# Weight blocks of two large experts placed between those of five small ones in the expert stage of a two-layer trunk, and the scatter of an expert's rows moved into the next unit

## The chip, the cores and the metric

The kernel runs on one core of one Trainium2 chip. The metric is the device time of one execution in microseconds, as the median of several runs. The kernel before took 1100.32 us (three runs, 1099.13 to 1101.1).

## The reference: what is computed

A trunk of two layers on 256 frames of 1024 channels, all in float32, batch 1. Layer 0 has attention and pooling with a dense SwiGLU, layer 1 a state-space mixer with a mixture of eight experts, and a norm ends it. Only the mixture matters here:

```
def swiglu(h, w1, w3, w2):
    return (jax.nn.silu(h @ w1) * (h @ w3)) @ w2

def moe_swiglu(h, router_w, router_b, w1, w3, w2):
    xf = h.reshape(b * s, d)                       # 256 x 1024
    top_vals, top_idx = lax.top_k(logits, TOP_K)   # 2 of 8
    gates = jax.nn.softmax(top_vals, axis=-1)
    ...
    for e in range(N_EXPERTS):
        ye = swiglu(xf, w1[e], w3[e], w2[e])       # D_FF = 2816
        out = out + combine[:, e:e + 1] * ye
# x = x + moe_swiglu(rms_norm(x)); the output is rms_norm(x)
```

## The kernel before, in words

All weights are streamed from device memory in tiles of 1 MB, each 128 partitions by 2048 values, by the queue of SP. The tiles go in turn into a ring of 17 buffers, all named raw here. An expert's weights are 33 tiles (`NBLK` is 11), so the eight experts make 264 loads.

**Rooms.** Instead of all 256 frames, an expert works on the frames that chose it, gathered into a fixed number of slots. The experts are renumbered by their counts (`by_count`): positions 0 to 5 have room for 64 frames and are called small, positions 6 and 7 have 128 and are called large. A loop behind the stage takes what doesn't fit; it isn't entered with these inputs. `Rows.gather` (L1212) makes the gathered rows x with one-hot matmuls, `Rows.scale` (L1226) the gates; `hold` does both for several experts at once. `hold([0], 64)` comes ahead of the stage, the one for the other small ones after unit 3 of expert 0, the one for the large ones after unit 3 of the next.

**Units.** The hidden width of 2816 is worked through in blocks of H = 512 (five of them) and one of 256. A full block has four tiles of w1 and w3 and two of w2, a half block three tiles. A small expert takes a block as one unit: 64 slots fill half of the columns of the array, which the profile shows as the shape 128*64. A large expert takes a full block as two half units of 256 hidden columns each, with 128 slots (128*128); both halves read the same four tiles, and each one tile of w2. A unit is

- `moe_in` (L1247): 16 steps over the channels into one PSUM bank p; then ScalarE (L1253) and VectorE (L1254) make g = silu(.) * (.) of 128x256 values;
- `moe_T` (L1261): two transposes of g into a bank t; ScalarE copies it to hT (L1263);
- `moe_out` (L1276): hT times w2, accumulated over the expert's units into one bank y (small) or two (large).

The function `turn` puts a unit's transposes into the middle of the next unit's `moe_in` (the argument `between`), and `tail` puts its `moe_out` behind that `moe_in`, so that ScalarE and VectorE have time for g and hT. The contexts `after(...)` only say what an instruction may not precede; the rest of the order on an engine is settled when the kernel is built, by when the build reckons that operands will be there.

**The end of an expert.** `slots_T` (L1284) transposes the one-hot matrix, `scatter` copies the banks y to SBUF as yf (ScalarE L1299 or L1302, VectorE L1300 or L1303) and multiplies by the one-hot matrix (L1312): frames 0 to 127 go into two banks y (`acc`) that are kept through the whole stage and were started with the residual x by `residual` (L1291); frames 128 to 255 go into two banks t, which VectorE adds to xt (L1316). In the last expert both halves are accumulated upon the residual in PSUM, and `final` (L1332 to L1355) works from there. PSUM has four banks y, two p and two t.

The experts run one after the other, in the order of positions 0, 1, 7, 2, 3, 6, 4, 5.

Of the kernel before, what the change touches and what calls it, by code (L numbers as in the profile page):

```python
# [20 lines left out]
NE = 8  # L21
# [7 lines left out]
NF = 5  # L29
# [9 lines left out]
def trunk_kernel(tc, x, par, cb, w_pool, wt, we, final_norm, out):  # L39
# [17 lines left out]
    with es:  # L57
# [1060 lines left out]
        order = [0, 1, 7, 2, 3, 6, 4, 5]  # L1118

# [174 lines left out]
        def scatter(PT, ys, acc, o1):  # L1294

            last = o1 is not None
            yf = tab.tile([128, 2, 512], F32, name="yf", tag="t2")
            if len(ys) == 1:
                sc.copy(yf[:, 0, 0:256], ys[0][:, 0:256])  # L1299
                ve.tensor_copy(yf[:, 0, 256:512], ys[0][:, 256:512])  # L1300
            else:
                sc.copy(yf[:, 0], ys[0])  # L1302
                ve.tensor_copy(yf[:, 1], ys[1])  # L1303
            o1 = o1 or [ttile(), ttile()]
            for tb, os in ((0, acc), (1, o1)):
                for nb in range(2):
                    if len(ys) == 1:
                        r = slice(64 * nb, 64 * nb + 64)
                        lhs, rhs = PT[r, tb], yf[r, 0]
                    else:  # L1310
                        lhs, rhs = PT[:, tb], yf[:, nb]
# [48 lines left out]
        def experts(todo, at):  # L1360

            acc = residual([ytile(), ytile()], 0)
            o1 = []
            prev = None

            def turn(st, behind):

                with after(behind):
                    st["h"] = moe_T(st["g"])
                return moe_T.last  # L1370

            def tail(st, B=None):
                n, u, h, ys, R, i, W = (st[k] for k in ("n", "u", "h", "ys", "R", "i", "W"))
                end = u == st["last"]
                moe_out(ys, h, B or [W.load(k) for k in st["B"]], R, u == 0, end)
                if end:
                    scatter(st["PT"], ys, acc, o1 if n == len(todo) - 1 else None)

            for n, p in enumerate(todo):
                W = Weights(p)  # L1380
                w = room(p) if len(todo) > 1 else 128

                units = []
                for t0 in range(0, 3 * NBLK, 6):
                    H = min(512, (3 * NBLK - t0) // 3 * 256)
                    if w == 64:
                        units.append((t0, H, 0, [t0 + H // 128 + k for k in range(H // 256)]))
                    else:
                        units += [(t0, H, h, [t0 + H // 128 + h]) for h in range(H // 256)]
                PT = None  # L1390
                for u, (t0, H, half, out_tiles) in enumerate(units):
                    if half == 0:
                        A = [W.load(t0 + s) for s in range(H // 128)]
                    if u == 0:
                        R, i = at(p)
                    g1 = moe_in(A, H, half, R, i, lambda mm: prev and turn(prev, mm))
                    if prev is not None:
                        with after(moe_in.last):
                            tail(prev)
                    if u == 0:  # L1400
                        ys = [ytile() for _ in range(w // 64)]
# [148 lines left out]
```

## Time and profile before

| | |
|---|---|
| median of three runs | 1100.32 us |
| the profiled execution | 1100.34 us |
| its span | 1098.3 us |
| PE busy, DMA | 97%, 311 GB/s over the span |
| expert stage (gather of expert 0 to the last scatter) | 433 to 1086 us |
| the two large experts | about 578 to 711 and 828 to 962 us |
| mean granted clock of TensorE | 0.99 of full speed |

The profile is of one execution. PE is the row of TensorE's matmuls, PEld that of its weight loads, DVE is VectorE, ACT ScalarE, POOL GpSimd, SP the engine whose queue issues the loads. The records of PE's matmuls carry modelled ends: a group's start is observed, its end lies a little beyond the start of the next one. Steps between starts are therefore the safe measure. A float32 matmul of the program shows as two matmuls (x8 for four) in the trace, a transpose as one. A square bracket behind a row gives the idle time ahead of it and what ended it.

### The profile page before, as it was taken

To read this page: it belongs to the slowest core of one execution; us is meant where nothing else is said; L and a number is where in the kernel's file an instruction comes from. 1 tells how busy PE (TensorE), PEld (TensorE's weight loads), DVE (VectorE), ACT (ScalarE), POOL (GpSimd) and SP (SyncE) were. 2 spreads that over 40 slices of the span, in tenths; PEclk is the share of its full clock that TensorE was granted. 3 is DMA by queue.
4 is the path that set the end of the run, shared out by engine and by line. 5 is a ranking of instruction groups with operands and counts; after the bars stand their busy time and mean duration, and the time that the engine had idled before them with its cause. 6 is when DMAs were issued, how large, how long until landed. Compare 5 with 4: busy or idle time off the path is not lost.

```text
span 1098.3 us, 13420 instructions
## 1 busy us (share of the span) xinstructions
PE 1061.1 (97%) x5139; PEld 606.6 (55%) x5139; DVE 388.1 (35%) x767; ACT 303.4 (28%) x563; POOL 139.0 (13%) x132
## 2 busy tenths in 40 slices
PE   8999999999999899999999999999998999999994
PEld 8977888888887778343343444333333444333331
DVE  6787968578779865110010000100100000000102
ACT  6474746644485551111010000000000000000101
POOL 2500999300003201000000000000000000000000
PEclk9999999999999999999999999999999999999998
DMA  6534545435443278799999987999999999999994
GB/s 248 228 115 154 189 156 192 154 116 208 161 148 136 78 295 356 322 427 425 428 425 428 427 320 317 420 407 427 426 427 427 428 426 384 387 387 426 427 425 164
DMA packets 48119, 341.63 MB, mean 311 GB/s; under 512 B 5296, under 2 KB 5936, under 8 KB 6832
## 3 DMA queue, kind: packets, MB, share of 16 engines
q1 hardware_dynamic: 47616, 340.02, 76.2%
q8 instruction: 42, 0.69, 0.2%
q10 hardware_dynamic: 432, 0.68, 0.2%
q14 instruction: 29, 0.24, 0.1%
HBM read 339.63 MB, written 1.05 MB: 310 GB/s over the span
## 4 chain that ended last, share of the span: by engine, by line
PE 74%; DMA 13%; DVE 5%; issue 4%; ACT 3%; POOL 1%; SPq 0%; POOLq 0%; ACTq 0%; DVEq 0%
PE p L1247 28%; PE y L1276 13%; DMA raw<-in_we_dram 12%; PE p L125 4%; PE p L126 4%; PE p L124 4%; PE y L124 4%; PE y L126 4%; PE y L125 4%; PE t L1261 1%; DVE hl L120 1%; PE t L1212 1%; ACT hl L119 1%; PE y L1312 1%; PE t L699 1%
## 5 line engine op out<-in xcount | busy, mean ns | idle before, releaser
L1247 PE MATMUL p<-raw,x 128*64 128x512 f32 (+2 forms) x1504 | 403.6, 575 | 1.9 <-DMA raw<-in_we_dram 1.9
L1247 PEld LDWEIGHTS p<-raw,x 128*64 128x64 f32 (+1 forms) x1504 | 144.7, 151 | 213.0 <-issue 196.6
L1254 DVE SCALAR_TENSOR_TENSOR g<-p,rs,g 128x256 f32<-128x256 f32 (+1 forms) x58 | 27.3, 470 | 541.0 <-ACT g L1253 541.0
L1276 PE MATMUL y<-raw,hT 128*64 128x512 f32 (+1 forms) x704 | 199.6, 594 | 2.0 <-DMA raw<-in_we_dram 1.4
L120 DVE TENSOR_TENSOR hl<-raw,hl 128x1024 fp32r<-128x1024 f32 x114 | 161.6, 1438 | 38.0 <-ACT hl L119 36.6
L119 ACT CAST hl<-raw 128x1024 fp32r<-128x1024 f32 x114 | 118.1, 1052 | 73.1 <-PE y L126 50.3
L1276 PEld LDWEIGHTS y<-raw,hT 128*64 128x64 f32 (+1 forms) x704 | 70.6, 150 | 119.2 <-issue 111.9
L1263 ACT COPY hT<-t 128x256 f32<-128x256 f32 (+1 forms) x58 | 20.9, 361 | 364.1 <-PE t L1261 364.1
L1338 POOL TENSOR_TENSOR fr<-fr,mhalf 128x1 f32<-128x1 f32 x2 | 1.1, 548 | 659.5 <-DVE fr L1337 659.5
L1253 ACT ACTIVATE g<-p,rs 128x256 f32<-128x256 f32 (+1 forms) x58 | 26.8, 462 | 176.8 <-PE p L1247 176.8
L124 PE MATMUL p<-hl,h1h 128*128 128x512 f32 x176 | 70.2, 399 | 0.1
L126 PE MATMUL p<-hl,h1l 128*128 128x512 f32 x176 | 69.3, 394 | 0.4 <-DVE h1l L207 0.4
L125 PE MATMUL p<-hl,h1h 128*128 128x512 f32 x176 | 69.6, 395 | 0.0
L126 PEld LDWEIGHTS p<-hl,h1l 128*128 128x128 f32 x176 | 33.1, 188 | 8.0 <-DVE h1l L207 0.9
L125 PEld LDWEIGHTS p<-hl,h1h 128*128 128x128 f32 x176 | 33.1, 188 | 7.1 <-DVE hl L120 0.3
L124 PEld LDWEIGHTS p<-hl,h1h 128*128 128x128 f32 x176 | 33.2, 188 | 6.6 <-ACT h1h L204 0.3
L1261 PEld LDWEIGHTS t<-ident,g 128*128 128x128 f32 x110 | 12.8, 141 | 40.3 <-issue 35.8
L124 PE MATMUL y<-hl,th 128*128 128x512 f32 x88 | 34.9, 396 | 0.0
L126 PE MATMUL y<-hl,tl 128*128 128x512 f32 x88 | 34.5, 393 | 0.0
L125 PE MATMUL y<-hl,th 128*128 128x512 f32 x88 | 34.2, 388 | 0.0
L124 PE MATMUL y<-h0h,hl 128*128 128x256 f32 x96 | 27.2, 284 | 0.0
L126 PE MATMUL y<-h0h,hl 128*128 128x256 f32 x96 | 27.2, 285 | 0.0
(406 smaller groups left out, 1247.0 us busy)
## 6 DMA issues: line engine op xcount, KB each, us to landing
raw<-in_we_dram SPq DMA_DIRECT2D x264, 1024.0 KB, 17.9
raw<-in_wt_dram SPq DMA_DIRECT2D x57, 1024.0 KB, 4.8
xt<-in_x_dram SPq DMA_DIRECT2D x2, 512.0 KB, 4.4
CB<-in_cb_dram SPq DMA_DIRECT2D x1, 1024.0 KB, 4.8
raw<-in_final_norm_dram SPq DMA_DIRECT2D x1, 512.0 KB, 18.3
out_dram<-raw SPq DMA_DIRECT2D x2, 256.0 KB, 3.5
out_dram<-raw ACTq DMA_DIRECT2D x2, 256.0 KB, 2.3
wpl<-in_w_pool_dram SPq DMA_DIRECT2D x1, 256.0 KB, 9.3
```

The costliest lines, as they stand in the source:

```text
L119: sc.copy(h.a[k][:, c], r[:, d])
L120: ve.tensor_sub(lo.a[k][:, c], r[:, d], f32(h.a[k][:, c]))
L124: pe.matmul(o, lh, rh, start=start, stop=False)
L125: pe.matmul(o, lh, rl, start=False, stop=False)
L126: pe.matmul(o, ll, rh, start=False, stop=stop)
L699: pe.matmul(t[0:32, k * 64:(k + 1) * 64], Bm[:, k, i].rearrange("p a b -> p (a b)"), Wu[:, c0 + k, i, 0:4].rearrange("p a b -> p (a b)"), ...
L1247: mm = pe.matmul(o[:, 0:2 * n].rearrange("p (w f) -> p w f", w=2), R.lhs(i, kc), a[:, kc % (KC // len(A)), :, h * n:h * n + n], start=kc = ...
L1253: sc.activation(g1, p[:, 0:n], AF.Silu, scale=R.rs[:, i, 0:1])
L1254: ve.scalar_tensor_tensor(g1, p[:, n:2 * n], R.rs[:, i, 1:2], g1, op0=OP.mult, op1=OP.mult)
L1261: moe_T.last = pe.transpose(t[:, f * 128:(f + 1) * 128], g1[:, f * 128:(f + 1) * 128], ident)
L1263: sc.copy(h, t[:, 0:n])
L1276: pe.matmul(o, h[:, j * w:j * w + w], B[c // 2][:, v:v + 512], start=first and c == 0, stop=last and c == m - 1)
```

## The change

The eight experts no longer run one after the other from position 1 on. `units` lists an expert's units; behind expert 0 the list `seq` takes the 30 units of experts 1 to 5 in turn, and spreads among them the 12 blocks of experts 7 and 6, each with its halves together. `experts` walks this list, with a small and a large expert under way at the same time, each with its banks y. The loads are issued in the same new order. Both holds now lie in expert 0, after its units 2 and 4.

`scatter` makes the copies yf as before, but hands back its matmuls as a function `add`, which `turn` calls behind the next unit's transposes. They go to two banks t and two banks y, and VectorE adds all four results to xt; no bank is kept for the sums. `residual` is called only at the end, for both halves of the frames, ahead of the last expert's scatter, which accumulates in PSUM as before. The loop for what doesn't fit is adapted. Line numbers of the stage's helpers are two lower (L1245, L1259, L1274, L1282, L1289, L1310, VectorE's adds L1313).

```diff
@@ -1115,8 +1115,6 @@
-        order = [0, 1, 7, 2, 3, 6, 4, 5]
...
@@ -1291,9 +1289,8 @@
-        def scatter(PT, ys, acc, o1):
-
-            last = o1 is not None
+        def scatter(PT, ys, sums):
+
             yf = tab.tile([128, 2, 512], F32, name="yf", tag="t2")
...
-            o1 = o1 or [ttile(), ttile()]
-            for tb, os in ((0, acc), (1, o1)):
-                for nb in range(2):
...
-                    pe.matmul(os[nb], lhs, rhs, start=tb == 1 and not last, stop=tb == 1 or last)
-            if not last:
-                for nb in range(2):
-                    xo = xt[:, 1, nb * 512:nb * 512 + 512]
-                    ve.tensor_add(xo, xo, o1[nb])
+            def add(banks):
+                for tb in range(2):
+                    for nb in range(2):
+                        o = sums[tb][nb] if sums else banks[tb]()
...
+                        i = pe.matmul(o, lhs, rhs, start=not sums, stop=True)
+                        if not sums:
+                            xo = xt[:, tb, nb * 512:nb * 512 + 512]
+                            ve.tensor_add(xo, xo, o)
+                return i
+
+            return add
...
@@ -1357,55 +1357,62 @@
-        def experts(todo, at):
-
-            acc = residual([ytile(), ytile()], 0)
-            o1 = []
...
+        def turn(st, behind):
+
+            with after(behind):
+                st["h"] = moe_T(st["g"])
+            if turn.left is None:
+                return moe_T.last
+            with after(moe_T.last):
+                i = turn.left((ttile, ytile))
+            turn.left = None
+            return i
...
+        def experts(seq, at, ahead):
+
             prev = None
...
                 if end:
-                    scatter(st["PT"], ys, acc, o1 if n == len(todo) - 1 else None)
...
+                    turn.left = scatter(e["PT"], e["ys"], sums)
+
+            for st in seq:
+                p = st["p"]
+                if st["u"] == 0:
+                    ex[p] = dict(W=Weights(p))
+                e = ex[p]
+                if st["half"] == 0:
+                    e["A"] = [e["W"].load(st["t0"] + s) for s in range(st["H"] // 128)]
...
+                st["g"] = moe_in(e["A"], st["H"], st["half"], e["R"], e["i"], lambda mm: prev and turn(prev, mm))
+                if prev is not None:
+                    with after(moe_in.last):
+                        tail(prev)
...
             turn(prev, moe_in.last)
-            o1 += residual([ttile(), ttile()], 1)
-            return prev, tail, [acc, o1]
+            return prev, tail, lambda k: ex[prev["p"]]["W"].load(k)
...
-            if (n, u) == (0, 3):
+            if (p, u) == (0, 2):
                 hold(list(range(1, NF + 1)), 64)
-            if (n, u) == (1, 3):
+            if (p, u) == (0, 4):
                 hold(list(range(NF + 1, NE)), 128)
...
+        few = [x for p in range(1, NF + 1) for x in units(p, 64)]
+        many = [x for p in range(NE - 1, NF, -1) for x in units(p, 128)]
+        blocks = sum(x["half"] == 0 for x in many)
+        seq = units(0, 64)
+        done = 0
+        for k, x in enumerate(few):
+            while many and done * len(few) <= k * blocks:
+                seq.append(many.pop(0))
+                while many and many[0]["half"]:
+                    seq.append(many.pop(0))
+                done += 1
+            seq.append(x)
         hold([0], 64)
-        prev, tail, sums = experts(order, at)
...
+        prev, tail, load_last = experts(seq, at, ahead)
...
-        tail(prev, B)
+        sums = [residual([f(), f()], tb) for tb, f in enumerate((ytile, ttile))]
+        tail(prev, B, sums)
+        turn.left(None)
```

How this moves PE's instructions at three places. In the rows, the number at a tile's name tells its buffers apart: p, g1, hT and y are those of a unit as above, t the bank of the transposes, raw a weight tile.

First, two units of a large expert amid its work, PE before:

```order
L1247 MATMUL p_4987<-raw_4979,x_4713 128x512 x2
L1247 MATMUL p_4987<-raw_4981,x_4713 128x512 x2
L1261 MATMUL t_4992<-ident_80,g1_4970 128x128 x2
L1247 MATMUL p_4987<-raw_4983,x_4713 128x512 x2
L1247 MATMUL p_4987<-raw_4985,x_4713 128x512 x2
L1276 MATMUL y_4900<-raw_5004,hT_4995 128x512
L1276 MATMUL y_4901<-raw_5004,hT_4995 128x512
L1276 MATMUL y_4900<-raw_5004,hT_4995 128x512
L1276 MATMUL y_4901<-raw_5004,hT_4995 128x512
L1247 MATMUL p_5010<-raw_4979,x_4713 128x512 x2
L1247 MATMUL p_5010<-raw_4981,x_4713 128x512 x2
L1261 MATMUL t_5015<-ident_80,g1_5001 128x128 x2
```

and a block of two halves with a small unit ahead of it, PE in the changed kernel:

```order
L1245 MATMUL p_4787<-raw_4779,x_4480 128x512 x2
L1245 MATMUL p_4816<-raw_4779,x_4480 128x512 x2
L1245 MATMUL p_4787<-raw_4781,x_4480 128x512 x2
L1259 MATMUL t_4792<-ident_80,g1_4764 128x128 x2
L1245 MATMUL p_4816<-raw_4781,x_4480 128x512 x2
L1245 MATMUL p_4787<-raw_4783,x_4480 128x512 x2
L1245 MATMUL p_4787<-raw_4785,x_4480 128x512 x2
L1259 MATMUL t_4821<-ident_80,g1_4801 128x128 x2
L1245 MATMUL p_4816<-raw_4783,x_4480 128x512
L1274 MATMUL y_4721<-raw_4804,hT_4795 64x512 x4
L1245 MATMUL p_4816<-raw_4783,x_4480 128x512
L1274 MATMUL y_4721<-raw_4806,hT_4795 64x512 x4
```

Before, g1_4970 is made in a moe_in; then a moe_out of four matmuls stands on PE (ahead of the first row), then half of the next moe_in, and then its transposes. Now p_4787 and p_4816, the two halves, take turns on the weight tiles; the transposes of g1_4801, which is made of p_4787, stand right behind the last matmul of p_4787, and the moe_out of the small unit (y_4721, 64 wide) lies amid the matmuls of the second half (128 wide).

Second, the end of a small expert (its last unit has a single transpose), PE before:

```order
L1261 MATMUL t<-ident,g_4505 128x128
L1247 MATMUL p<-raw,x 64x512 x8
L1276 MATMUL y<-raw,hT 64x512 x4
L1312 MATMUL y<-yf,PT 128x512 x2
L1312 MATMUL t<-yf,PT 128x512 x2
L1247 MATMUL p<-raw,x 64x512 x8
L1261 MATMUL t<-ident,g_4552 128x128 x2
```

and in the changed kernel:

```order
L1259 MATMUL t<-ident,g_5014 128x128
L1245 MATMUL p<-raw,x 64x512 x8
L1274 MATMUL y<-raw,hT 64x512 x4
L1245 MATMUL p<-raw,x 64x512 x8
L1259 MATMUL t<-ident,g_5055 128x128 x2
L1310 MATMUL t<-yf,PT 128x512 x2
L1310 MATMUL y<-yf,PT 128x512 x2
L1245 MATMUL p<-raw,x 64x512 x8
```

The scatter (L1312, now L1310) has moved from directly behind its own moe_out of four matmuls to behind the next unit's transposes, eight matmuls of moe_in later.

Third, the end of the stage, PE before:

```order
L1261 MATMUL t<-ident,g_6547 128x128 x2
L1247 MATMUL p<-raw,x 64x256 x8
L1261 MATMUL t<-ident,g_6593 128x128
L1291 MATMUL t<-xt,ident 128x512
L1276 MATMUL y<-raw,hT 64x512 x4
L1291 MATMUL t<-xt,ident 128x512
L1276 MATMUL y<-raw,hT 64x512 x8
L1312 MATMUL y<-yf,PT 128x512 x2
L1312 MATMUL t<-yf,PT 128x512 x2
```

and in the changed kernel:

```order
L1245 MATMUL p<-raw,x 64x256 x8
L1274 MATMUL y<-raw,hT 64x512 x4
L1259 MATMUL t<-ident,g_6617 128x128
L1274 MATMUL y<-raw,hT 64x512 x4
L1289 MATMUL y<-xt,ident 128x512 x2
L1289 MATMUL t<-xt,ident 128x512 x2
L1274 MATMUL y<-raw,hT 64x512 x4
L1310 MATMUL y<-yf,PT 128x512 x2
L1310 MATMUL t<-yf,PT 128x512 x2
```

The residual (L1291, now L1289) has four matmuls here in place of two; the scatter stays behind the last moe_out.

## Rows read from the trace of the kernel before

**Rows 1.** The page of the profiled execution: its span, the busy time of the engines, the chain that ended last by engine and its costliest lines, and the issues of the expert weights (KB each, median us from issue to landing).

```profile
span 1098.3 us, 13420 instructions
...
PE 1061.1 (97%) x5139; PEld 606.6 (55%) x5139; DVE 388.1 (35%) x767; ACT 303.4 (28%) x563; POOL 139.0 (13%) x132
...
PE 74%; DMA 13%; DVE 5%; issue 4%; ACT 3%; POOL 1%; SPq 0%; POOLq 0%; ACTq 0%; DVEq 0%
PE p L1247 28%; PE y L1276 13%; DMA raw<-in_we_dram 12%; PE p L125 4%; PE p L126 4%; PE p L124 4%; PE y L124 4%; PE y L126 4%; PE y L125 4%; PE t L1261 1%; DVE hl L120 1%; PE t L1212 1%; ACT hl L119 1%; PE y L1312 1%; PE t L699 1%
...
raw<-in_we_dram SPq DMA_DIRECT2D x264, 1024.0 KB, 17.9
```

**Rows 2.** Busy time by stretches of the expert stage. Columns: the stretch and its length, then busy us and number of instructions of PE, PEld, DVE, ACT and POOL, the granted clock of TensorE, the mean busy share of the DMA engines, and GB/s. In 593:711 and 845:962 a large expert runs, in the others small ones.

```profile
521.00:593.00 72.00, 71.07 (x335) 28.33 (x333) 6.39 (x14) 7.35 (x18) 0.00 (x0) 1.00 1.01 427
593.00:711.00 118.00, 117.23 (x308) 51.12 (x306) 7.99 (x15) 10.26 (x24) 0.00 (x0) 1.00 0.92 376
...
845.00:962.00 117.00, 117.00 (x306) 50.93 (x306) 7.32 (x14) 10.12 (x24) 0.00 (x0) 1.00 0.98 407
962.00:1070.00 108.00, 105.53 (x501) 35.44 (x498) 6.49 (x14) 9.16 (x23) 0.00 (x0) 1.00 1.00 417
```

**Rows 3.** The same view for three stretches of 10 us, the first behind the first hold, the others in a large expert.

```profile
484.00:494.00 10.00, 10.00 (x55) 6.16 (x54) 1.82 (x4) 1.24 (x3) 0.00 (x0) 0.83 1.01 426
650.00:660.00 10.00, 10.00 (x26) 4.47 (x25) 0.48 (x1) 0.85 (x2) 0.00 (x0) 1.00 0.53 202
670.00:680.00 10.00, 10.00 (x26) 4.55 (x25) 0.48 (x1) 0.84 (x2) 0.00 (x0) 1.00 0.44 162
```

**Rows 4.** What the queue of SP waited for in 590 to 711 us: engine, line, what released it, us in total, times, the longest.

```profile
SPq L1179 <- PE p L1247: 52.8, 17, 11.7
```

**Rows 5.** What PE waited for in 453 to 1086 us, in the same columns.

```profile
PE y L1312 <- DVE yf L1300: 5.6, 6, 0.9
PE p L1247 <- DMA raw<-in_we_dram: 1.9, 3, 0.6
PE t L1261 <- DVE xt L1316: 1.5, 2, 0.8
PE y L1276 <- DMA raw<-in_we_dram: 1.4, 3, 0.6
```

**Rows 6.** PE's timeline over a unit of a small expert: start, modelled duration, line, operation, array shape and tile, count. moe_in is on L1247, the transposes on L1261, moe_out on L1276.

```profile
732.66 3.60 PE L1247 MATMUL p<-raw,x 128*64 128x512 f32 x16
736.20 0.44 PE L1261 MATMUL t<-ident,g 128*128 128x128 f32 x2
...
743.48 3.60 PE L1247 MATMUL p<-raw,x 128*64 128x512 f32 x16
```

**Rows 7.** The same over one half of a large expert.

```profile
601.18 3.60 PE L1247 MATMUL p<-raw,x 128*128 128x512 f32 x8
...
611.70 3.60 PE L1247 MATMUL p<-raw,x 128*128 128x512 f32 x8
```

**Rows 8.** The same where a small expert gives way to a large one.

```profile
574.26 3.60 PE L1276 MATMUL y<-raw,hT 128*64 128x512 f32 x16
577.80 5.42 PE L1247 MATMUL p<-raw,x 128*128 128x512 f32 x12
583.05 0.27 PE L1261 MATMUL t<-ident,g 128*128 128x128 f32 x1
583.16 5.32 PE L1247 MATMUL p<-raw,x 128*128 128x512 f32 x12
```

**Rows 9.** The timeline at the end of a large expert: the last eight moe_out matmuls; the second group of scatter matmuls, which starts behind those eight and the first four of scatter.

```profile
703.72 3.70 PE L1276 MATMUL y<-raw,hT 128*128 128x512 f32 x8
...
709.16 1.88 PE L1312 MATMUL t<-yf,PT 128*128 128x512 f32 x4
```

**Rows 10.** The timeline at the end of the stage, where the last unit's transposes follow their moe_in directly (PE, ACT and DVE rows).

```profile
1072.38 1.95 PE L1247 MATMUL p<-raw,x 128*64 128x256 f32 x16
...
1074.37 0.37 ACT L1253 ACTIVATE g<-p,rs 128x128 f32<-128x128 f32 x1 [1.56 <-PE p L1247]
1074.77 0.35 DVE L1254 SCALAR_TENSOR_TENSOR g<-p,rs,g 128x128 f32<-128x128 f32 x1 [9.15 <-ACT g L1253]
...
1075.18 0.33 PE L1261 MATMUL t<-ident,g 128*128 128x128 f32 x1 [0.85 <-DVE g L1254]
...
1075.34 1.02 PE L1291 MATMUL t<-xt,ident 128*128 128x512 f32 x2
```

**Rows 11.** Groups of instructions of one line and shape in 453 to 1070 us: count, then busy us and mean ns of one, then idle time before them and what ended it.

```profile
L1276 PE MATMUL y<-raw,hT 128*64 128x512 f32 x504 | 114.6, 594 | 2.0 <-DMA raw<-in_we_dram 1.4 <-ACT g L1253 0.6
...
L1254 DVE SCALAR_TENSOR_TENSOR g<-p,rs,g 128x256 f32<-128x256 f32 x51 | 24.7, 484 | 489.2 <-ACT g L1253 489.2
L1253 ACT ACTIVATE g<-p,rs 128x256 f32<-128x256 f32 x51 | 24.1, 473 | 160.9 <-PE p L1247 160.9
...
L1316 DVE TENSOR_TENSOR xt<-xt,t 128x512 f32<-128x512 f32 x14 | 9.2, 685 | 14.9 <-PE t L1312 14.9
```

**Rows 12.** The timeline at the end of the first hold.

```profile
486.40 2.29 PE L1226 MATMUL t<-rgp,P 128*128 128x2 f32 x20
```

**Rows 13.** PE's timeline at the start and the end of the expert stage.

```profile
433.09 0.40 PE L1212 MATMUL t<-P,xh 128*128 128x64 f32 x2 [0.20 <-DVE P L1195]
...
1084.77 1.02 PE L1312 MATMUL t<-yf,PT 64*128 64x512 f32 x4
```

More of the change, by code (lines that the diff above doesn't have):

```diff
@@ L1358, in final @@
             return norm
-        def experts(todo, at):
-            acc = residual([ytile(), ytile()], 0)
-            o1 = []
-            prev = None
[L1366 to L1375, printed above, removed]
-                if end:
-                    scatter(st["PT"], ys, acc, o1 if n == len(todo) - 1 else None)
[L1379 to L1401, printed above, removed]
-                    prev = dict(n=n, u=u, last=len(units) - 1, g=g1, ys=ys, R=R, i=i, W=W, PT=PT, B=out_tiles)
-                    if u == len(units) - 2:
-                        PT = slots_T(R, i)
-                    ahead(n, u)
@@ new lines, in units @@
+        def units(p, w):
+            us = []
+            for t0 in range(0, 3 * NBLK, 6):
+                H = min(512, (3 * NBLK - t0) // 3 * 256)
+                out = [t0 + H // 128 + k for k in range(H // 256)]
+                us += [dict(t0=t0, H=H, half=0, B=out)] if w == 64 else \
+                    [dict(t0=t0, H=H, half=h, B=out[h:h + 1]) for h in range(H // 256)]
+            return [dict(x, p=p, w=w, u=i, n=len(us)) for i, x in enumerate(us)]
+        def turn(st, behind):
[7 more added lines that the diff above has]
+            return i
@@ new lines, in trunk_kernel, with tail @@
+        turn.left = None
+        def experts(seq, at, ahead):
+            prev = None
+            ex = {}
+            def tail(st, B=None, sums=None):
+                e = ex[st["p"]]
+                end = st["u"] == st["n"] - 1
+                if st["u"] == 0:
+                    e["ys"] = [ytile() for _ in range(st["w"] // 64)]
+                moe_out(e["ys"], st["h"], B or [e["W"].load(k) for k in st["B"]], e["R"], st["u"] == 0, end)
+                if end:
+                    turn.left = scatter(e["PT"], e["ys"], sums)
+            for st in seq:
+                p = st["p"]
+                if st["u"] == 0:
+                    ex[p] = dict(W=Weights(p))
+                e = ex[p]
+                if st["half"] == 0:
+                    e["A"] = [e["W"].load(st["t0"] + s) for s in range(st["H"] // 128)]
+                if st["u"] == 0:
+                    e["R"], e["i"] = at(p)
+                st["g"] = moe_in(e["A"], st["H"], st["half"], e["R"], e["i"], lambda mm: prev and turn(prev, mm))
+                if prev is not None:
+                    with after(moe_in.last):
+                        tail(prev)
+                prev = st
+                if st["u"] == st["n"] - 2:
+                    e["PT"] = slots_T(e["R"], e["i"])
+                ahead(p, st["u"])
@@ L1442, in count @@
                                   skip_runtime_bounds_check_because="a count of T tokens at most")
-        def ahead(n, u):
-            pass
         def keep(sums):
@@ L1453, in trunk_kernel @@
         with tc.If(count(NE) > 0):
-            for p in order:
+            for p in range(NE):
                 for k in range(0, most(p) - room(p), 128):
```

22 lines of the change are left out of this document (12 added, 10 removed).

## The prediction

> **What bounds the kernel now.** I read the page first, then the stretches of the expert stage (about 434 to 1085 us), then what PE waits for there, then single units in the timeline. The page gives two answers. Its chain of waits puts 13% on DMA, 12% of it on the expert weights, while PE is busy for 97% of the span [rows 1]. By stretches the transfers do run at 427 GB/s with a share of 1.01 wherever small experts run, but they fall to 0.92 and 0.98 in the two stretches of the large ones [rows 2]; two 10-us stretches inside the first show 0.53 and 0.44 [rows 3], and SP stands there because PE hasn't freed a buffer [rows 4]. So the weights are early there and just in time elsewhere. What decides is how long PE stands: in 633 us it waits 1.9 + 1.4 = 3.3 us for weights, and 5.6 us for the copies of a finished expert's rows [rows 5]. Elsewhere its matmul steps follow each other at 3.43 us for 16 half-width or 8 full-width passes, 0.429 us for a full-width one. The stage is TensorE's, with the transfers close behind: 264 tiles [rows 1] of 1 MB at 427 GB/s, 2.456 us each, are 648 us, against 652 us of PE from the first gather to the last scatter (433.09 to 1085.6, [rows 13]).
>
> So the question is what the change does to PE's own row of instructions. Spreading the large blocks can give back only PE's waits, some 10 us; what it adds to PE's row comes off that.
>
> **Unit times.** A small unit takes 743.48 - 732.66 = 10.82 us [rows 6], a large half 611.70 - 601.18 = 10.52 [rows 7]. Both hold the same 24 x 0.429 = 10.29 us of passes, and both one pair of transposes. The pair costs 0.23 us amid a large half, where every matmul uses the array as 128x128, and 0.53 amid a small unit, where the array goes from 128x64 to 128x128 and back. Two changes of shape cost 0.30 us, **0.15 each**. The two single steps that show one are 3.54 in place of 3.43 (0.11) where moe_out of a small unit gives way to a large one, and from there to the end of the transpose 583.16 - 574.26 = 8.90 against 3.43 + 5.15 + 0.11 = 8.69 (0.21) [rows 8]. These are my bounds: 0.11 and 0.21.
>
> **What goes.**
> - *Scatter waits.* Six small experts end with their copies in PE's way, 5.6 / 6 = 0.93 us each [rows 5]. The new order puts the four matmuls behind the next unit's transposes. It does so for all but two (expert 0's, and one more whose moe_out the build put right ahead) and the last, which ends the stage as before. Three go: 2.8 us. At a large expert's end, twelve passes take 709.16 - 703.72 = 5.44 in place of 5.15 [rows 9]: two more times 0.3. Together -3.4.
> - *Transposes behind VectorE's adds*, twice: -1.5 [rows 5].
> - *Weights:* -3.3 [rows 5]. Once PE's stage is longer than the 648 us of transfers, and large blocks (six tiles, 14.7 us of transfers, 21.0 us of PE) stand between small units (14.7 against 10.8), no run of small units is long enough to use up the filled buffers. If half of this stays, it is -1.7.
> - A matmul's modelled end hides part of each pause: a matmul's record lasts 0.594 [rows 11] at a step of 0.429, so 0.16 for each of 11 waits: -1.8.
>
> Sum -10.0; at the least -7.
>
> **What comes.**
> - *Half 0's transposes.* Before, a half's transposes stand a whole moe_out behind their moe_in (3.43 us, which covers ScalarE's and VectorE's work on g). Now both halves of a block are mixed tile by tile, and half 0's transposes stand directly behind the last matmul of half 0, nine times; PE is in order, so all behind them waits. The one place before where transposes follow their moe_in directly is the end of the stage: 0.85 us behind the modelled end, for a g of 128 columns [rows 10]. With 256 columns, ScalarE takes 0.47 for 0.37 and VectorE 0.48 for 0.35 [rows 10, 11], so 1.09, and with the hidden 0.16 1.25. Nine times: **+11.3**. Lower bound 0.85 (7.7); upper 1.62, with a copy of hT (0.37) in ScalarE's way (14.6).
> - *Changes of shape.* A block with two halves now adds six of them (eight in and around it, less two at transposes that now lie among 128x128 matmuls), and in the stage's whole row I count some 65 more: x 0.15 = **+9.8** (7.2 to 13.7). The Trainium skill ("TensorEngine Tiling (Array Packing)", Key Properties) says that a change of tiling mode drains TensorE, and gives no price; by that rule every change would cost the same, which the 0.11 and 0.21 here don't bear out or refute.
> - *Residual.* All four matmuls with the identity now stand at the end. Two stood there before, each of two passes (one of them in [rows 10]); two more are 4 x 0.43 = +1.7. What they leave ahead of the stage lay beside other work (0 to -0.7).
> - *VectorE* adds four pieces of 0.685 us per expert where it added two [rows 11]: 14 more, 9.6 us, on an engine busy for 8 us of 118 [rows 2]. The 2.7 us of one scatter lie beside the next 3.43 us of moe_in, before moe_out wants a bank. If that cover went, the next moe_out would wait under 1 us. Nothing.
> - *Holds moved*, the small one by one unit, the large one by five, both now in expert 0: the same gathers, with the transfers running ahead meanwhile. Nothing, but for the clock (below). The loads have the same number and size, and SP issues them in the new order; it waits for buffers, not PE for SP.
>
> Sum +22.8. Net **+12.8** on the profiled execution (1100.34 us, span 1098.3 [rows 1]), which stands on the median of the runs (1100.32): **1113 us**. All low bounds with all gains: 7.7 + 7.2 + 1.0 - 10.0 = +5.9, 1106. All high with the small gain: 14.6 + 13.7 + 1.7 - 7 = +23, 1123.
>
> **Rivals.**
> 1. *Faster, at 1090.* The transfers are the bound, and PE's seeming busyness follows them. Then the idle time of the transfers comes back: 8% of 118 us and 2% of 117 [rows 2], 11.7 us; with the 1.7 of the residual 1090. It decides if the new pauses of PE fall where PE would have waited for weights anyway, which needs more than 22 us of such waits. Against it: 3.3 us of them are shown, and the steps of 0.429 hold in stretches with and without full transfers. The Trainium skill ("Perfetto Trace Analysis", Identifying the Most-Contended Engine and Optimization Strategy) points this way: it calls matmul busy time a poor measure, wants the busy share of weight loads (here 35.44 of 108 us in the last stretch [rows 2]), and says that interleaving stages with different limits may help. The rows bear out the two kinds of stage, but not the headroom: **10%**.
> 2. *One of the two losses doesn't appear*, because a change of shape is hidden by a weight load, or the scalar work finishes earlier than in rows 10: +12.8 - 9.8 = 1103, or - 11.3 = 1102. Against it: the 0.30 of a small unit repeats, and nothing covers the transposes in the order: **10%**.
> 3. *Slower still.* TensorE's granted clock is 0.83 in one stretch of 10 us behind the first hold [rows 3], that is 3.4 us at 1.2 GHz in place of 2.4; ahead of it stood 20 matmuls of two columns each [rows 12]. It cost 1.7 us. The second hold has been given a like place, unmixed with moe_in, and nine pauses are new. One more is 1115; nine more 1128: **7%**, with the upper part of my own bounds.
> 4. *No change:* the change plainly moves the instructions, so this needs gains and losses to cancel, at 1100: **4%**.
>
> **How the numbers follow.** The forecast has 69%: 1113, its own range 1106 to 1123. For 8 in 10 the range goes down to take in most of rival 2 and up to one or two clock dips: 1103 to 1122. A measurement of this kernel tells about 0.2%, 2.2 us, from no change. Faster: rival 1, 0.10. Same (1098.1 to 1102.5): rival 4 and a part of rival 2, 0.08. Slower: the rest, 0.82.
>
> **What would show it.** In the profile after: PE waiting at the transposes for VectorE's g about nine times, 0.9 to 1.2 us each; waits for weights and nearly all for yf gone; the share of the transfers below 1 evenly through the stage, in place of full and half-empty stretches; around a block single steps longer by 0.1 to 0.2. I am wrong if PE waits for weights by more than 5 us, if these transposes don't wait, or if the stage gets shorter.

## The result, and the profile after

The changed kernel takes **1115.14 us** (median of four runs, 1113.98 to 1116.43) where the kernel before, run beside it, takes 1099.91: a ratio of 1.0138, 95% interval 1.0120 to 1.0155. It is slower by 15.2 us. The profiled execution has a span of 1113.7 us, 15.4 more than before, so its rows can be set against those of before as they are.

The page first: the lines that answer to [rows 1].

```profile
span 1113.7 us, 13434 instructions
...
PE 1075.6 (97%) x5139; PEld 603.3 (54%) x5139; DVE 396.8 (36%) x781; ACT 303.4 (27%) x563; POOL 138.6 (12%) x132
...
PE 86%; DVE 5%; issue 4%; ACT 3%; POOL 1%; DMA 0%; ACTq 0%; POOLq 0%; DVEq 0%
```

PE is still busy for 97% of the span, but now with 14.5 us more. Of the 13% that the chain of waits gave to DMA nothing is left: the weights are never late, and the kernel is slower. What PE waits for now, from the head of the stage to its end (in all, times, longest):

```profile
PE t L1259 <- DVE g L1252: 9.8, 9, 1.1
PE t L1310 <- DVE yf L1297: 1.9, 2, 0.9
PE y L1310 <- DVE yf L1297: 1.0, 1, 1.0
```

Set against [rows 5], the waits for weights are gone, the waits for yf have fallen from 5.6 to 2.9 us, and nine waits for VectorE's g stand in the first line, 1.1 us each. The stretches of [rows 2]:

```profile
521.00:593.00 72.00, 68.90 (x243) 24.72 (x242) 6.29 (x12) 5.92 (x14) 0.00 (x0) 1.00 0.99 407
593.00:711.00 118.00, 115.83 (x431) 42.19 (x431) 7.61 (x15) 9.26 (x23) 0.00 (x0) 1.00 1.01 423
...
845.00:962.00 117.00, 113.90 (x438) 41.57 (x435) 8.10 (x16) 9.49 (x24) 0.00 (x0) 1.00 1.00 416
962.00:1070.00 108.00, 106.92 (x389) 40.09 (x389) 7.62 (x15) 8.98 (x22) 0.00 (x0) 1.00 0.98 408
```

The transfers are even: 407 to 423 GB/s in all four, where before they went from 376 to 427. They also finish earlier: the last weight tile has landed at 1071.5 us, 29 us ahead of the stage's end, before at 1079.7, 5 us ahead of it. The spread has done to the transfers just what it should.

Then a block of two halves, PE's timeline (start, modelled duration; moe_in is L1245, the transposes L1259, moe_out L1274):

```profile
616.76 5.42 PE L1245 MATMUL p<-raw,x 128*128 128x512 f32 x12
622.02 0.38 PE L1259 MATMUL t<-ident,g 128*128 128x128 f32 x2
622.24 5.32 PE L1245 MATMUL p<-raw,x 128*128 128x512 f32 x12
628.63 0.44 PE L1259 MATMUL t<-ident,g 128*128 128x128 f32 x2 [1.08 <-DVE g L1252]
628.91 1.02 PE L1245 MATMUL p<-raw,x 128*128 128x512 f32 x2
629.86 1.94 PE L1274 MATMUL y<-raw,hT 128*64 128x512 f32 x8
631.73 1.13 PE L1245 MATMUL p<-raw,x 128*128 128x512 f32 x2
632.79 1.94 PE L1274 MATMUL y<-raw,hT 128*64 128x512 f32 x8
634.65 1.98 PE L1245 MATMUL p<-raw,x 128*128 128x512 f32 x4
636.48 3.60 PE L1274 MATMUL y<-raw,hT 128*128 128x512 f32 x8
640.00 1.95 PE L1245 MATMUL p<-raw,x 128*64 128x256 f32 x16
```

From 622.24 twelve full-width passes should take 5.15 us; the next row starts 6.39 us later, so 1.25 us are lost at one pair of transposes. Who it is shows in the other engines' rows of the same place:

```profile
627.59 0.47 ACT L1251 ACTIVATE g<-p,rs 128x256 f32<-128x256 f32 x1 [4.73 <-PE p L1245]
628.09 0.48 DVE L1252 SCALAR_TENSOR_TENSOR g<-p,rs,g 128x256 f32<-128x256 f32 x1 [13.66 <-ACT g L1251]
```

ScalarE and VectorE need 0.47 and 0.48 us for g, with the handing on between, and PE has only the transposes of that g at the head of its queue. Behind it, moe_out of the small unit is cut in two by a full-width matmul pair: every row from 629.86 to 640.00 changes the array's shape against the one ahead of it, save the one at 636.48.

For the sum over the stage I take each step between the starts of two groups of PE's rows, less the count of its matmuls times 0.429 us (full width; half of it for 64 wide, a quarter for 64 wide with 256 columns), for transposes 0.108 each, between the first gather and the last scatter:

| us | before | after | difference | the prediction's term |
|---|---|---|---|---|
| stage | 652.1 | 667.8 | +15.7 | +12.8 |
| nine waits for g, 1.25 each | 0 | 11.3 | +11.3 | +11.3 |
| steps that change the shape (88, then 160), the 0.11 that follows a way into full width, and small rests | 15.2 | 27.5 | +12.3 | +9.8 |
| waits for weights (one of them put down to ScalarE) | 5.4 | 0 | -5.4 | -3.3, and some of -1.8 |
| scatters behind their moe_out | 6.8 | 3.5 | -3.3 | -3.4 |
| moved scatters, beyond their passes | 0 | 2.3 | +2.3 | 0 |
| transposes behind xt, and those at the stage's end | 3.2 | 0 | -3.2 | -1.5 |
| residual's matmuls | | | +1.7 | +1.7 |
| gather and half clock | 23.4 | 23.3 | -0.1 | 0 |

The 88 and the 160 leave out those changes of shape whose step is a wait, or lies in a gather. All changes of the stage, counted in PE's rows, are 106 before and 171 after: 65 more. The residual's 1.7 is the count of its matmuls times 0.429.

### The profile page after: what moved, and what is told of

Read it like the earlier page. It is cut to its first block, busy times and chain, and to the rows that moved or that the text cites. A ratio compares the mean times of both kernels' runs of the same rounds, so it can differ in the third digit from the quotient of the medians.

```text
span 1113.7 us, 13434 instructions
## 1 busy us (share of the span) xinstructions
PE 1075.6 (97%) x5139; PEld 603.3 (54%) x5139; DVE 396.8 (36%) x781; ACT 303.4 (27%) x563; POOL 138.6 (12%) x132
## 3 DMA queue, kind: packets, MB, share of 16 engines
HBM read 339.63 MB, written 1.05 MB: 306 GB/s over the span
## 4 chain that ended last, share of the span: by engine, by line
PE 86%; DVE 5%; issue 4%; ACT 3%; POOL 1%; DMA 0%; ACTq 0%; POOLq 0%; DVEq 0%
PE p L1245 36%; PE y L1274 17%; PE p L125 4%; PE p L126 4%; PE p L124 4%; PE y L126 4%; PE y L124 4%; PE y L125 4%; PE t L1259 2%; DVE hl L120 1%; PE t L1210 1%; PE t L1310 1%; PE y L1310 1%; ACT hl L119 1%; PE t L699 1%
## 5 line engine op out<-in xcount | busy, mean ns | idle before, releaser
L1245 PE MATMUL p<-raw,x 128*64 128x512 f32 (+2 forms) x1504 | 407.3, 576 | 0.0
L1245 PEld LDWEIGHTS p<-raw,x 128*64 128x64 f32 (+1 forms) x1504 | 141.0, 150 | 226.9 <-issue 218.2
L1274 PE MATMUL y<-raw,hT 128*64 128x512 f32 (+1 forms) x704 | 202.4, 597 | 0.0
L1274 PEld LDWEIGHTS y<-raw,hT 128*64 128x64 f32 (+1 forms) x704 | 68.4, 150 | 121.2 <-issue 115.0
L1261 ACT COPY hT<-t 128x256 f32<-128x256 f32 (+1 forms) x58 | 20.9, 361 | 323.3 <-PE t L1259 323.3
L1259 PEld LDWEIGHTS t<-ident,g 128*128 128x128 f32 x110 | 12.1, 141 | 50.4 <-issue 32.4
L1259 PE MATMUL t<-ident,g 128*128 128x128 f32 x110 | 24.0, 296 | 9.8 <-DVE g L1252 9.8
L124 PE MATMUL y<-h0h,hl 128*128 128x256 f32 x96 | 27.2, 283 | 0.0
```

What stands on the lines that cost most here:

```text
L124: pe.matmul(o, lh, rh, start=start, stop=False)
L1245: mm = pe.matmul(o[:, 0:2 * n].rearrange("p (w f) -> p w f", w=2), R.lhs(i, kc), a[:, kc % (KC // len(A)), :, h * n:h * n + n], start=kc = ...
L1259: moe_T.last = pe.transpose(t[:, f * 128:(f + 1) * 128], g1[:, f * 128:(f + 1) * 128], ident)
L1261: sc.copy(h, t[:, 0:n])
L1274: pe.matmul(o, h[:, j * w:j * w + w], B[c // 2][:, v:v + 512], start=first and c == 0, stop=last and c == m - 1)
```

## The experiments

All were timed against the kernel before on the same chip; the ratios are those to it. Where one kernel is set against another, it is by these ratios or by the stage's length in the profiles.

**The halves of a block kept apart.** Theory: PE's own row has grown by waits and changes of shape. Rivals: the transfers, or the new adds of VectorE.

```diff
...
+                    moe_out.last = pe.matmul(...)
...
-                st["g"] = moe_in(...)
+                with after(*([behind] if st["half"] and behind else [])):
+                    st["g"] = moe_in(...)
...
                     with after(moe_in.last):
                         tail(prev)
+                    behind = moe_out.last
```

> The changed kernel with one edge more: the second half of a large block is queued behind the moe_out of the unit ahead of the block, so that the two halves no longer share the weight tiles in turns. In the order no transposes stand directly behind their moe_in (nine before), two of the three scatters that stood directly behind their moe_out are covered, and TensorE changes its array shape 14 times less. Theory (the loss is in TensorE's own row): -9 x 1.25 - 14 x 0.15 - 2 x 1.1 = -15.5, so 1099 to 1101 us, no wait for VectorE's g left, none for weights. Rival (the loss comes from the spread as such, through the transfers or the new adds of VectorE): within 3 us of the changed kernel, 1112 to 1116, the pauses showing up as waits for weights or for xt. Rival (only the changes of shape cost): about 1113.

Measured: 1101.08 us, ratio 1.0015 (1.0002 to 1.0028). Of the 1.38% of loss 1.23 are gone with one edge in the order. The stage is 652.4 us. What is left of its waits, and the place of a block:

```profile
PE y L1310 <- DVE yf L1297: 1.0, 1, 1.0
```

```profile
573.59 3.60 PE L1245 MATMUL p<-raw,x 128*128 128x512 f32 x8
577.12 3.65 PE L1274 MATMUL y<-raw,hT 128*64 128x512 f32 x16
580.70 3.70 PE L1245 MATMUL p<-raw,x 128*128 128x512 f32 x8
584.24 0.38 PE L1259 MATMUL t<-ident,g 128*128 128x128 f32 x2
```

The transposes at 584.24 now stand a moe_out and half a moe_in behind the moe_in at 573.59 that made their g, and the small unit's moe_out is in one piece at 577.12. The spread, the loads and the adds are those of the changed kernel; so neither the transfers nor VectorE's adds were the loss.

**The waits alone.** That run takes away waits and changes of shape together. This one leaves the halves mixed and lets the transposes wait less.

```diff
-                if kc == KC // 2:
+                if kc == (3 * KC // 4 if half else KC // 2):
```

> The changed kernel with one number changed: in the second half of a large block the transposes of the first half may come only after three quarters of the moe_in, not after half of it. The halves still share the weight tiles in turns, and the count of changes of shape is the same (174 for 173), so it takes a part of the nine waits alone: one full-width matmul of 0.86 us then lies between the first half's last matmul and its transposes. Theory (wait of 1.25 us each, 0.86 of it covered): -9 x 0.86 = -7.7 us against the changed kernel and one direct scatter less, -1.1, so 0.4 to 0.7% above before (1.004 to 1.007), with nine waits for g of about 0.2 to 0.4 us left. Rival (the mixing of the halves costs by its changes of shape or by its transfers, the waits would be there anyway): as the changed kernel, 1.012 to 1.0155.

Measured: 1106.29 us, ratio 1.0058 (1.0035 to 1.0081), the middle of the forecast; the stage is 659.4 us, 8.4 shorter than in the changed kernel (-8.8 expected). The waits are as forecast: by the starts of PE's rows they cost 8.1 us less. The direct scatter that was to go is still there, with a wait shorter by 0.4. The group ahead of the transposes is longer by the passes that cover them:

```profile
PE t L1259 <- DVE g L1252: 1.8, 8, 0.2
```

```profile
574.77 7.03 PE L1245 MATMUL p<-raw,x 128*128 128x512 f32 x16
582.03 0.33 PE L1259 MATMUL t<-ident,g 128*128 128x128 f32 x1 [0.23 <-DVE g L1252]
582.28 1.94 PE L1274 MATMUL y<-raw,hT 128*64 128x512 f32 x8
```

**The price of a change of shape alone**, with no wait in it: the two transposes of a small unit a quarter of the moe_in apart.

```diff
-                if kc == KC // 2:
-                    done = between(mm)
+                if kc in (KC // 2, 3 * KC // 4):
+                    done = between(mm, kc > KC // 2, R.w)
...
+            fs = range(n // 128) if second is None else [int(second)]
```

> The kernel with the halves apart, and inside every moe_in of a small unit the two transposes of the unit before put a quarter of the moe_in apart: the same instructions, 62 more changes of the array's shape by the count of the order (221 for 159). It measures the price of a change by itself. Theory (0.15 us each): 9.3 us above the kernel with the halves apart. Bounds 0.11 and 0.21: 7 to 13. Rival (a change is hidden by the weight load, and the steps read in the trace were something else): within 2 us of it.

Measured: 1107.22 us, ratio 1.0078 (1.0049 to 1.0107). Against the halves apart that is 0.63%, 6.9 us, a little under the lower bound. The profiles say why: the stage is 7.6 us longer (660.0 against 652.4). In it the steps that change shape are 63 more and 9.5 us longer, 0.15 each; 2.1 us came back because the half clock behind the first hold did not appear in this execution (below). A place of it:

```profile
699.28 3.65 PE L1247 MATMUL p<-raw,x 128*64 128x512 f32 x16
702.87 0.33 PE L1263 MATMUL t<-ident,g 128*128 128x128 f32 x1
703.12 1.94 PE L1247 MATMUL p<-raw,x 128*64 128x512 f32 x8
704.99 0.33 PE L1263 MATMUL t<-ident,g 128*128 128x128 f32 x1
705.25 1.94 PE L1247 MATMUL p<-raw,x 128*64 128x512 f32 x8
707.02 3.60 PE L1280 MATMUL y<-raw,hT 128*64 128x512 f32 x16
```

From 699.28 to 707.02 are 7.74 us for 6.86 of passes and 0.22 of transposes: 0.66 for four changes, 0.16 each. The rival (a change is hidden by the weight load) falls.

**The spread alone**, the scatter directly behind its moe_out.

```diff
-                    turn.left = scatter(e["PT"], e["ys"], sums)
+                    add = scatter(e["PT"], e["ys"], sums)
+                    if sums:
+                        turn.left = add
+                    else:
+                        add((ttile, ytile))
```

> The spread alone: the changed kernel with an expert's scatter directly behind its last moe_out, as before the change, all four results still added by VectorE. The order then has seven transposes directly behind their moe_in in place of nine, and eight scatters behind their moe_out in place of three. Theory: -2 x 1.25 + 3 x 1.1 (small) + 2 x 0.3 (large) + up to 2 for transposes behind VectorE's adds, less the 3 x 0.6 of array changes that the moved scatter makes: 1115 to 1118 us; moving the scatter is worth next to nothing. Rival (the move of the scatter and its adds is where the time went): 1105 or less. Rival (it hid much more than the waits shown): over 1120.

Measured: 1113.85 us, ratio 1.0131 (1.0103 to 1.0160): not told apart from the changed kernel's 1.0138, and a little under what I expected. The waits behind VectorE's adds, for which I had allowed up to 2 us, don't show. Its waits:

```profile
PE t L1259 <- DVE g L1252: 7.6, 7, 1.1
PE t L1310 <- DVE yf L1297: 4.7, 5, 0.9
```

Three more waits for yf have come back (4.7 us for 1.9), and two for g have gone. Moving the scatter saves a wait of 1.1 us and pays part of it back at once. The changed kernel at such a place:

```profile
660.33 0.44 PE L1259 MATMUL t<-ident,g 128*128 128x128 f32 x2
660.70 1.28 PE L1310 MATMUL t<-yf,PT 64*128 64x512 f32 x3
661.66 0.59 PE L1310 MATMUL y<-yf,PT 64*128 64x512 f32 x1
661.82 0.59 PE L1310 MATMUL t<-yf,PT 64*128 64x512 f32 x1
662.09 1.18 PE L1310 MATMUL y<-yf,PT 64*128 64x512 f32 x3
663.20 3.65 PE L1245 MATMUL p<-raw,x 128*64 128x512 f32 x16
```

Eight matmuls whose passes are worth 1.72 us take 663.20 - 660.70 = 2.50, between transposes of one shape and a moe_in of another. At three places of before they took 1.92, here 773.94 - 772.02:

```profile
772.02 1.13 PE L1312 MATMUL y<-yf,PT 64*128 64x512 f32 x4 [0.93 <-DVE yf L1300]
772.99 1.02 PE L1312 MATMUL t<-yf,PT 64*128 64x512 f32 x4
773.94 3.65 PE L1247 MATMUL p<-raw,x 128*64 128x512 f32 x16
```

I didn't have this in the sum, and my expectation of this run put it down to changes of shape. A scatter at its old place has as many of them. The rows of ScalarE and of the weight loads at the moved scatter show another cause:

```profile
660.86 0.37 ACT L1261 COPY hT<-t 128x256 f32<-128x256 f32 x1 [3.47 <-PE t L1259]
661.28 0.18 PEld L1310 LDWEIGHTS t<-yf,PT 64*128 64x128 f32 x1 [0.29 <-ACT hT L1261]
```

The scatter takes both banks t, and one of them still holds the transposes that stand just ahead of it. The weight load for that bank waits until ScalarE has copied hT out of it, at 661.23; its matmul starts 0.58 us behind the first one. All three moved scatters of small experts show this wait, with the same 0.58 to 0.59. So 1.7 us of the 2.3 in the table are a wait that the move itself has made. A third bank t for the scatter would test it; no run does.

**The scatter alone**, the experts in turn as before the change.

```diff
-        few = ...
-        ...
+        seq = [x for p in (0, 1, 7, 2, 3, 6, 4, 5) for x in units(p, room(p))]
```

> The scatter alone: the changed kernel with the experts one after the other in the order of before (0, 1, 7, 2, 3, 6, 4, 5), both holds in expert 0. The order has three transposes directly behind their moe_in (before: one), three scatters behind their moe_out (before: eight), 101 changes of shape (before, counted alike: 108; changed kernel: 173). Theory: against before -3 x 1.1 - 2 x 0.3 - 2.1 (transposes behind xt) + 2 x 1.25 + 1.7 (residual) = about -2, part of it given back as waits for weights in the small experts: 1097 to 1102 us. Rival (transfers pace the small experts): 1100 with longer waits for weights, 8 us or more. Rival (the new scatter is the loss): 1110 or more.

Measured: 1096.39 us, ratio 0.9976 (0.9962 to 0.9989). The time is a little under my range. The kernel with the moved scatter gains a little where the experts run in turn, so the move isn't the loss. Waits for weights are 2.3 us, fewer than before: neither rival.

**In turn, with the halves apart**: both edits above together.

> The moved scatter with the experts one after the other, and the halves of a block apart: against the kernel with the experts in turn two direct transposes less (-2.5) and two direct scatters less (-2.2), 103 changes of shape. Theory: TensorE's row gets 4.7 us shorter, but it runs more of the small experts ahead of their weights, and the waits for weights (2.3 us shown with the experts in turn) grow by about 1 to 2 us: 0.994 to 0.997 of before. Rival (the transfers pace the small experts in a row): the whole 4.7 come back as waits for weights, 0.9976 as with the experts in turn.

Measured: 1096.30 us, ratio 0.9964 (0.9952 to 0.9975), in the range of the theory. But the runs don't tell it from the experts in turn (0.9962 to 0.9989), and so hardly from the rival. The profile says that little is gained: the waits for the transposes fall by 2.5 us and those for the scatters by 2.3, and nearly all of this comes back.

```profile
PE p L1245 <- DMA raw<-in_we_dram: 2.4, 5, 0.6
PE y L1274 <- DMA raw<-in_we_dram: 1.0, 2, 0.6
...
PE y L1274 <- ACT g L1251: 0.6, 1, 0.6
```

Shown are 2.4 + 1.0 = 3.4 us of waits for weights in place of 2.3. The 0.6 put down to ScalarE are another: PE starts at 834.64, and the tile has landed at 834.51. By the starts of PE's rows, less the changes of shape, the waits for weights cost about 6 us in place of 3. Two more moved scatters cost 1.4. So most of the 4.8 us comes back, in part as the rival had it. This is the place where the transfers begin to bind: small experts in a row.

**Coarser spreads.** With the halves apart, the twelve blocks as six pairs:

```diff
-                seq.append(many.pop(0))
-                while many and many[0]["half"]:
-                    seq.append(many.pop(0))
-                done += 1
+                for _ in range(2):
+                    seq.append(many.pop(0))
+                    while many and many[0]["half"]:
+                        seq.append(many.pop(0))
+                    done += 1
```

> The kernel with the halves apart, and the twelve large blocks placed as six pairs, a pair ahead of every five small units, in place of twelve single ones. 28 changes of shape less (131 for 159), one transpose directly behind its moe_in more. Theory: each way into the large shape costs about 0.2 and each way back 0.15, so -28 x 0.17 + 1.25 = -3.5 against the kernel with the halves apart, which was 0.15% above before: 0.2% below before (0.997 to 1.000), still no wait for weights. Rival (the spread must be fine to help, or the weights fail): waits for weights appear, no gain.

Measured: **1094.45 us, ratio 0.9953** (0.9939 to 0.9968): faster than before and than the changed kernel, and better than I expected. The stage is 646.8 us, 5.7 less than with single blocks. 5.1 of it are changes of shape (28 fewer, 0.18 each), 1.05 were paid for the transposes at the end, and 1.6 are gather and clock at the head of the stage, which differ from one execution to the next. No wait for weights stands in its list, and none in the chain of waits:

```profile
PE 87%; DVE 5%; issue 4%; ACT 3%; POOL 1%; DMA 0%; POOLq 0%; ACTq 0%; DVEq 0%
```

How much of this gain is the spread's is not shown. The kernel with the experts in turn and the halves apart has 0.9964, and the two intervals overlap. Against it the pairs save about 6 us of waits for weights and pay for 28 more changes of shape (129 for 101).

The same with `range(3)`, four groups of three blocks:

> The same with four groups of three blocks, seven or eight small units between them. 41 changes less than with single blocks (118 for 159). Theory: -41 x 0.17 + 1.25 = -5.7, so 0.4% below before (0.995 to 0.998), the buffers of 17 tiles just bridging 7.5 small units (each takes 3.9 us longer to load than to work), with at most 1 to 2 us of waits for weights. Rival (weights fail over such a stretch): waits above 4 us, and no better than pairs.

Measured: 1099.01 us, ratio 0.9992 (0.9979 to 1.0006). My forecast fails: the buffers do not bridge seven or eight small units.

```profile
PE p L1245 <- DMA raw<-in_we_dram: 2.2, 5, 0.6
PE y L1274 <- ACT g L1251: 1.2, 2, 0.6
...
PE y L1274 <- DMA raw<-in_we_dram: 0.8, 2, 0.4
```

The two lines with DMA show 3.0 us of waits for weights; the 1.2 put down to ScalarE are for weights too (PE goes on at 937.75, the tile has landed at 937.61). By the starts of PE's rows they cost about 6 us together, above the 4 of the rival, and with them the gain of 13 fewer changes is gone: the stage is 650.7 us, 4.0 longer than with the pairs. Of the three spreads tried the middle one is the best: fine enough that the weights hold out, coarser than single blocks, so that the array changes its shape less often.

**The half clock behind the first hold.** In most profiles TensorE's granted clock falls to 1.2 GHz for about 3.4 us there, behind twenty two-column matmuls [rows 12]. Here they stand ahead of the gather in both holds.

```diff
-            R = Rows(ps, w).gather()
+            R = Rows(ps, w)
             if ps[0] == 0:
+                R.gather()
                 gates()
-            R.scale()
+                R.scale()
+            else:
+                R.scale().gather()
```

> The kernel of the run before this one, with the two-column matmuls of both holds ahead of their gathers in place of behind. It tests what stands ahead of TensorE's half clock for 3.4 us behind the first hold. If the twenty two-column matmuls bring it on, it now falls into the gather or vanishes: up to -1.7 us. If it is any work of that kind, or comes and goes by itself: no difference over 1 us.

Measured: 1094.80 us, ratio 0.9956 (0.9939 to 0.9974), to be set against 0.9964 of the kernel without the edit. The stretch in which the gather lies, without and with the edit (the granted clock is the column ahead of the DMA share):

```profile
470.00:485.00 15.00, 15.00 (x82) 9.28 (x80) 2.37 (x5) 2.48 (x5) 0.00 (x0) 0.89 1.01 427
```

```profile
470.00:485.00 15.00, 15.00 (x90) 9.48 (x90) 2.37 (x5) 2.48 (x5) 0.00 (x0) 1.00 1.01 427
```

The half clock is gone, and the stage is 3.1 us shorter in the profile. The half clock had cost 1.7 of them, by the length of the one moe_in that it covered; the rest lies at the head of the stage and in waits for weights. The intervals of the ratios overlap. The same edit upon the pairs:

> The six pairs of blocks with the halves apart (0.9953 of before), and the two-column matmuls of both holds ahead of their gathers. Expected: the half clock behind the first hold is gone in the profile, and 1 to 1.7 us less: 0.993 to 0.995 of before. Rival (the half clock comes and goes by itself): no difference from the pairs.

Measured: 1093.60 us, ratio 0.9951 (0.9935 to 0.9967) against 0.9953. Again the profile has no half clock in that stretch, and again the runs don't tell the two apart. Of the ten profiles with the two-column matmuls behind the gather nine have the half clock there, of the two with them ahead of it none. The exception is the kernel with the split transposes. That these matmuls bring it on is likely and not shown, and what it is worth in the median stays open.

## Why the prediction was right

**The bound.** It was TensorE's own row, and not the transfers that the chain of waits named. The changed kernel shows it by the plainest means: waits for weights gone, DMA at 0% of the chain, 15 us slower.

**Half 0's transposes** were priced from one row at the end of the stage, widened by two group means and the part that a modelled end hides: 1.25 us. The rows show 1.25, nine times. Here the mechanism and the size were both right.

**Changes of shape** is the mis-sized term: 9.8 predicted, 12.3 measured, with the count right and the price not. 0.15 came from transposes amid a small unit, and holds there (the split transposes: 0.15). The new changes are mostly between long groups, and there the way into full width costs more than the way back: 0.10 at the change and another 0.11 at the end of the first full-width group, against 0.10 and 0.05. Both stand in the rows of the halves apart: 580.70 to 584.24 are 3.54 us for 3.43 of passes, with no change at their end, and 577.12 to 580.70 are 3.58 with one. The step from 574.26 to 583.16 in [rows 8] had shown the 0.21, and I took it for a bound only. So the changes don't all cost alike. The 72 steps of the table cost 0.17 each on average; they are more than 65 because some changes that fell into a wait or a gather before now stand alone.

**What goes** was -10.0; without the moved scatters it is -11.9, larger at the weights (5.4 by starts, 3.3 + 1.0 in the sum) and at the last transposes, whose wait of 0.85 us [rows 10] fell away because the new order has half a moe_out ahead of them; I had seen that row only as a price. The moved scatters took 2.3 back, the one cost with no term in the sum. I had put their matmuls behind the transposes without asking when the bank t comes free. Residual +1.7, VectorE's adds nothing (no wait for xt is left), holds nothing: as predicted.

The remaining error, +15.4 against +12.8 in the profiled execution, is 2.5 for shape and 2.3 for the moved scatters, less some 2 more of gains. So two costs were too low and the gains too low as well; that the sum came as near as it did is in part luck. One sign was off: I expected a share of the transfers below 1, and it is 0.98 to 1.01.

**The rivals.** The first (transfers bind, 1090) is out for this kernel. It wasn't empty: the waits for weights that it wanted back do go, and the pairs keep that at a lower price (0.9953). The Trainium skill ("Perfetto Trace Analysis", Optimization Strategy) says that interleaving stages whose limits differ may improve performance. Here the single blocks made the kernel slower, and the pairs are not told apart from the experts in turn (0.9964). As a measure of TensorE's headroom the Trainium skill ("Perfetto Trace Analysis", Identifying the Most-Contended Engine) names the busy share of weight loads, beside another. In the changed kernel it is 42 of 118 us in a stretch in which PE was busy for 115.8 of them, so it doesn't show that PE had little time to give. The second rival is out by two runs, each of which shows one of the two losses alone. The third, more half clock, did not come: one such stretch at the first hold, as before.

## What to carry to other kernels

When two kinds of work are interleaved to even out transfers, read the order that the build makes of it, engine by engine, before the times: an instruction whose operands come from another engine needs other work between it and its producer, and a scheduler that mixes two halves to be early with one can take just that away. Price what an in-order engine gains in instructions, waits and reconfigurations against the waits that it loses, which are often only a few microseconds however long the chain of waits names them. When work is moved, ask also which buffer it will want at its new place, and who still holds it. And once the order is sound, look for the coarsest grain that still keeps the buffers filled, and time it against no interleaving at all.

## What the runs showed of the hardware

A change of TensorE's array shape costs 0.15 to 0.16 us around short transposes (9.5 us for 63 steps). Between long float32 groups it costs about 0.21 on the way from 128x64 to 128x128 and about 0.15 on the way back. The Trainium skill ("TensorEngine Tiling (Array Packing)", Key Properties) says that changing the tiling mode drains TensorE; the price is what these runs add.

Within the runs of one kernel a longer time goes with a lower clock of TensorE. With the halves apart, the ten runs have mean granted clocks of 0.985 to 0.990 and times of 1102.03 to 1098.59 us: the one with 0.990 is the fastest, those with 0.985 and 0.986 are four of the five slowest. The same holds for the pairs (0.987: 1097.3 and 1097.7 us; 0.991: 1093.0 and 1093.6). One stretch of half clock cost 1.7 us, so two profiles can differ by that much without any difference between their kernels.
